# Half-swap of an 8192x8192 matrix: all row copies from GpSimd, each DMA over 8 rows a step

## The chip, the core and the metric

The kernel runs on one core of one Trainium2 chip. A core has five instruction engines (TensorE, VectorE, ScalarE, GpSimd and SyncE) and 16 DMA engines. This kernel computes nothing: its instruction engines only issue DMAs, and the DMA engines do the work.

The metric is device time in microseconds (us), from launch to end, as the median of several runs. Before the change it is 812.07 us, the median of 3 runs (811.68, 812.07, 814.06).

## What is computed

```python
x = np.random.randn(8192, 8192).astype(np.float32)
def reference(x):
    return np.fft.ifftshift(x)
```

With 8192 rows and columns, ifftshift moves every element by 4096 rows and 4096 columns, around the edges. So the four quadrants swap in pairs along the diagonals. Half a row (4096 float32 values, 16 KiB) stays together: the left half of output row r is the right half of input row (r + 4096) mod 8192, and the right half of output row r is the left half of that input row. A whole row is 32 KiB, each matrix 268.44 MB.

## The kernel before, in words

Nothing passes through on-chip memory: each DMA copies from the input in HBM to the output in HBM. `copy(queue, row, col, dims)` (L26) issues one DMA on the engine it is given as `queue`; the profile puts every DMA at L29, the line of that `dma_start`. Source and destination have the same three dimensions, `dims`, and differ only in their offset.

- The innermost dimension is the 4096 values of half a row: one packet of 16,384 bytes.
- The outermost dimension is 16 neighbouring rows (`ENGINES`), a row apart.
- Between them stands a dimension of `per` = 16 steps. Each step goes 16 rows back, so a DMA begins at the last 16 rows of its block and works towards its first ones.

So one DMA moves half a row of each of 16 x 16 = 256 rows (`rows`), which is 4 MiB in 256 packets. There are 64 DMAs: 32 blocks of 256 rows, each with a left and a right half.

The order of the work is written out by hand. The outer loop takes 4 blocks at a time and goes from the end of the matrix to its beginning. Within 4 blocks the left halves go in the order 3, 2, 1, 0, and the right halves in the order 1, 0, 3, 2: a left DMA and the right DMA issued beside it lie two blocks (512 rows) apart. Left halves are issued by SyncE (`nc.sync`, L38), right halves by ScalarE (`nc.scalar`, L39), 32 DMAs each. `ENGINES` is set ahead of the function, `per` in L23, and `dims` is `back` of L34.

No DMA depends on another. The framework gives each DMA one of eight completion semaphores in turn, four on each of the two engines. So from its fifth DMA on, each engine waits, before it issues, until the DMA four places earlier in its own order has landed. Eight DMAs are in flight, 4 left and 4 right. When a DMA is complete, each of its 16 parts has added one to the semaphore.

GpSimd does four small MEMSETs of constants at the start (L54, put there by the framework) and nothing else.

Of the kernel before, what the change touches and what calls it, by code (L numbers as in the profile page):

```python
# [1 line left out]

# [4 lines left out]


ENGINES = 16


@with_exitstack
def kernel(
    ctx: ExitStack,
    tc: tile.TileContext,
    x: bass.AP,
    out: bass.AP,
):
    nc = tc.nc
    R, C = x.shape  # L20
    hr = R // 2
    hc = C // 2
    per = 16  # L23
    rows = ENGINES * per

    def copy(queue, row, col, dims):  # L26

        src = (row + hr) % R * C + (col + hc) % C
        queue.dma_start(  # L29
            out=bass.AP(out.tensor, out.offset + row * C + col, dims),  # L30
            in_=bass.AP(x.tensor, x.offset + src, dims),
        )

    back = [[C, ENGINES], [-ENGINES * C, per], [1, hc]]  # L34

    for first in range(R - 4 * rows, -1, -4 * rows):
        for n in (3, 2, 1, 0):
            copy(nc.sync, first + n * rows + rows - ENGINES, 0, back)  # L38
            copy(nc.scalar, first + (n + 2) % 4 * rows + rows - ENGINES, hc, back)  # L39


# [1 line left out]
_INS = ['x']  # L43
_OUTS = [((8192, 8192), 'float32')]


def kernel(**inputs):
    import numpy as _np
    import concourse.bacc as _bacc
    import concourse.tile as _tile  # L50
    from concourse import mybir as _mybir
    from concourse.bass_utils import run_bass_kernel_spmd as _run

    nc = _bacc.Bacc("TRN2", target_bir_lowering=False, num_devices=1)  # L54
    arrays, args = {}, []
    for name in _INS:
        a = _np.ascontiguousarray(inputs[name])
        if a.dtype.kind in "iu":
            a = a.astype(_np.int64)
        arrays[f"in_{name}_dram"] = a  # L60
        args.append(nc.dram_tensor(f"in_{name}_dram", a.shape, _mybir.dt.from_np(a.dtype), kind="ExternalInput").ap())
    for i, (shape, dtype) in enumerate(_OUTS):
        dt = _mybir.dt.from_np(_np.dtype(dtype))
        args.append(nc.dram_tensor(f"out_{i}_dram", shape, dt, kind="ExternalOutput").ap())
    with _tile.TileContext(nc) as tc:
        kernel(tc, *args)
    r = _run(nc, [arrays], core_ids=[0])
    got = tuple(r.results[0][f"out_{i}_dram"] for i in range(len(_OUTS)))
    return got[0]
```

## Time and profile before

| | before |
|---|---|
| median of 3 runs | 812.07 us (811.68 to 814.06) |
| the profiled execution's own time | 813.9 us |
| span in that profile, first to last instruction | 812.1 us |
| bytes read from HBM, and written | 268.44 MB, 268.44 MB |
| packets | 17,408: 16,384 of 16 KiB, 1,024 of 4 bytes (semaphore updates) |
| first issue / first packet starts / last packet ends, in the span | 0.73 / 2.18 / 810.9 us |

The rows of the profile are read so. The "DMA" digits give, for each of 40 slices of the span, the mean busy share of the 16 DMA engines in tenths (9 is 90% or more). "GB/s" gives what was copied in that slice; each byte copied is read once and written once. A DMA queue's row ("q1", "q10") gives its packets, its bytes and the time of its packets as a share of 16 engines' span. An issue row gives how many DMAs an engine issued, their size, and the median time from the issue to the landing of the last byte. "SPq" and "ACTq" are the issuing sides of SyncE and ScalarE, and "POOL" is GpSimd. In the records of the trace, the 4-byte semaphore packets of q1 fall on the landings of SyncE's DMAs and those of q10 on ScalarE's, so q1 carries the left halves and q10 the right halves.

### The profile page before, as it was taken

To read this page: it belongs to the slowest core of one execution; us is meant where nothing else is said; L and a number is where in the kernel's file an instruction comes from. 1 tells how busy PE (TensorE), PEld (TensorE's weight loads), DVE (VectorE), ACT (ScalarE), POOL (GpSimd) and SP (SyncE) were. 2 spreads that over 40 slices of the span, in tenths; PEclk is the share of its full clock that TensorE was granted. 3 is DMA by queue.
4 is the path that set the end of the run, shared out by engine and by line. 5 is a ranking of instruction groups with operands and counts; after the bars stand their busy time and mean duration, and the time that the engine had idled before them with its cause. 6 is when DMAs were issued, how large, how long until landed. Compare 5 with 4: busy or idle time off the path is not lost. (4 is left out here: it accounts for less than half of the span.)

```text
span 812.1 us, 109 instructions
## 1 busy us (share of the span) xinstructions
POOL 0.2 (0%) x4
## 2 busy tenths in 40 slices
POOL 0000000000000000000000000000000000000000
DMA  9999999999999999999999999999999999999998
GB/s 306 332 329 337 333 332 335 328 324 337 329 336 337 332 334 334 334 336 331 332 329 330 337 328 334 339 331 333 332 320 333 330 331 330 336 332 337 334 333 286
DMA packets 17408, 268.44 MB, mean 331 GB/s; under 512 B 1024, under 2 KB 1024, under 8 KB 1024
## 3 DMA queue, kind: packets, MB, share of 16 engines
q1 hardware_dynamic: 8704, 134.22, 49.9%
q10 hardware_dynamic: 8704, 134.22, 49.1%
HBM read 268.44 MB, written 268.44 MB: 661 GB/s over the span
## 5 line engine op out<-in xcount | busy, mean ns | idle before, releaser
L54 POOL MEMSET const-bfloat16-1.0<- 128x1 bf16 x1 | 0.1, 102 | 0.0
L54 POOL MEMSET const-uint8-127<- 128x1 uint8 x1 | 0.1, 102 | 0.0
L54 POOL MEMSET const-float32-1.0<- 128x1 f32 x1 | 0.1, 99 | 0.0
L54 POOL MEMSET const-float32-0.0<- 128x1 f32 x1 | 0.1, 98 | 0.2 <-issue 0.2
## 6 DMA issues: line engine op xcount, KB each, us to landing
out_dram<-in_x_dram ACTq DMA_DIRECT2D x32, 4096.0 KB, 101.0
out_dram<-in_x_dram SPq DMA_DIRECT2D x32, 4096.0 KB, 101.0
```

The source lines that it names most:

```text
L54: nc = _bacc.Bacc("TRN2", target_bir_lowering=False, num_devices=1)
```

## The change

`ENGINES` goes from 16 to 8 and `per` from 16 to 32, so `rows` stays 256 and a DMA still moves 256 half rows, now as 32 steps of 8 neighbouring rows. All 64 DMAs are issued by GpSimd (`nc.gpsimd`), in one order: left half, right half, left half, and so on. Which blocks stand beside each other stays as it was. SyncE and ScalarE issue nothing.

```diff
-ENGINES = 16
+ENGINES = 8
...
-    per = 16
+    per = 32
     rows = ENGINES * per
...
     back = [[C, ENGINES], [-ENGINES * C, per], [1, hc]]
     for first in range(R - 4 * rows, -1, -4 * rows):
         for n in (3, 2, 1, 0):
-            copy(nc.sync, first + n * rows + rows - ENGINES, 0, back)
-            copy(nc.scalar, first + (n + 2) % 4 * rows + rows - ENGINES, hc, back)
+            copy(nc.gpsimd, first + n * rows + rows - ENGINES, 0, back)
+            copy(nc.gpsimd, first + (n + 2) % 4 * rows + rows - ENGINES, hc, back)
```

In the built kernel the DMAs of SyncE and ScalarE (16x16x4096, 32 on each) become 64 of 8x32x4096 on GpSimd. The first eight are issued without a wait; every later one waits for the DMA eight places before it, by eight semaphores in turn. So again eight are in flight, 4 left and 4 right, but the waits now stand in one order on one engine.

## The prediction

> **What bounds the kernel now.** I read the page from the top. Its first part has only four MEMSETs on GpSimd, 0.2 us; so the DMA rows carry everything.
>
> ```profile
> span 812.1 us, 109 instructions
> DMA  9999999999999999999999999999999999999998
> GB/s 306 332 329 337 333 332 335 328 324 337 329 336 337 332 334 334 334 336 331 332 329 330 337 328 334 339 331 333 332 320 333 330 331 330 336 332 337 334 333 286
> DMA packets 17408, 268.44 MB, mean 331 GB/s; under 512 B 1024, under 2 KB 1024, under 8 KB 1024
> q1 hardware_dynamic: 8704, 134.22, 49.9%
> q10 hardware_dynamic: 8704, 134.22, 49.1%
> HBM read 268.44 MB, written 268.44 MB: 661 GB/s over the span
> out_dram<-in_x_dram ACTq DMA_DIRECT2D x32, 4096.0 KB, 101.0
> out_dram<-in_x_dram SPq DMA_DIRECT2D x32, 4096.0 KB, 101.0
> ```
>
> The reader should see three things. The 16 DMA engines are busy in every slice (99.0% in sum, 49.9 + 49.1). The rate hardly moves: between the ramps of the first and last slice it lies between 320 and 339 GB/s. And no issue is late: 64 DMAs in 812.1 us are one per 12.7 us, and eight of them in flight make 101 us, which is the landing time in the last two rows; a DMA stands in a queue for nearly all of its life.
>
> Busy is not the same as at full speed. In the packet records a 16 KiB packet takes 0.608 us at the least, a third of the packets (33%) take under 0.616 us, the median is 0.726 and the mean 0.784 us. (These are read from the trace's record of each packet.) At 0.611 us throughout, 16 engines would need 16,384 x 0.611 / 16 = 626 us. So the engines are held up by something they share, by 28% on the mean. The bytes read and written together, 661 GB/s, pass through the HBM; I take that as the bound.
>
> The windows show that it is steady, and that the end is short:
>
> ```profile
> core 0: us, POOL busy (x), PEclk, DMA share, GB/s
> 0.00:20.00 20.00, 0.20 (x4) 1.00 0.91 307
> 100.00:200.00 100.00, 0.00 (x0) 1.00 0.99 331
> 400.00:500.00 100.00, 0.00 (x0) 1.00 1.00 332
> 700.00:800.00 100.00, 0.00 (x0) 1.00 0.99 333
> 807.00:812.10 5.10, 0.00 (x0) 1.00 0.43 138
> ```
>
> On the Trainium skill's page "HBM Reference", section "Specifications (TRN2)", one HBM domain gives about 716 GB/s. The 661 of the row are 92% of it; by that figure alone 536.9 MB would need an estimated 750 us, so it speaks against any large gain from a change of order, and no run here shows how near one can come.
>
> **The change, part by part.**
>
> *Which engines carry a DMA.* The whole change rests on it, and the trace of before does not show it: every DMA there has 16 rows a step and its 16 semaphore updates. The bounds are two. If left and right DMAs go to different eights of engines, all 16 stay in work, and nothing is lost. If both go to the same eight, each of these has 2 x 1024 packets at no less than 0.611 us, 1251 us. I take the first: in the trace the 16 rows of a step are dealt out so evenly that no engine falls behind (below), which is nearer to 64 DMAs shared by two eights than to one eight left idle.
>
> Here the skill speaks on both sides. "DMA: Bandwidth & Descriptors" says under "Rules for kernel authors" that an outermost dimension below 16 confines a DMA to at most that many engines, which speaks against the change; and under "Why a DMA increments its semaphore by 16 and not by 1" that SyncE's and ScalarE's DMAs take the lowest-numbered engines, but GpSimd's the next ones in turn from a moving cursor. By the first alone the sum would be 1251 us, by both together it is the one that follows. No row of this trace decides between them.
>
> *Removed: 32 issues on SyncE, 32 on ScalarE.* They were never late (each waited for a landing with three more of its DMAs queued), so taking them away gains nothing.
>
> *Added: 64 issues on GpSimd, and waits in one order.* GpSimd has nothing else to do after its MEMSETs. Behind a waiting issue stand all later DMAs of both halves. But DMA i+8 waits for DMA i, and when that one lands its engines still have three DMAs queued, 3 x 32 packets x 0.784 = 75 us. So a late half stops the other only when it is some 75 us behind. What GpSimd needs to prepare a DMA of 256 packets has no row. From below: no more than SyncE, whose first issue in the trace takes 0.67 us. From above: if each packet cost as much as a MEMSET (0.10 us), 25.6 us per DMA. Up to 12.7 us per DMA it is hidden, except before the first packets. Of the two I take the row of the same operation, 0.67 us, as the nearer; the other end is a rival.
>
> *Moved: left halves on eight engines, right halves on the other eight.* Today every engine carries both, so all 16 finish together: the 16 updates of a DMA lie 1.1 us apart at the first landing and 2 to 3 us at the last ones. That also says that no engine is slower than another by more than 3 us in 810. What differs is the kind of copy: a left packet takes 0.791 us, a right one 0.778. On halves of their own:
> - left: 49.9% x 2 x 812.1 = 810.5 us of packets on each of its eight engines
> - right: 49.1% x 2 x 812.1 = 797.5 us
> - gaps: packets fill 804.0 us of the 808.7 between the first packet's start (2.18) and the last one's end (810.9). The last updates lie 2 us apart, so up to 2 us of this are ragged ends; I keep 3 us of gaps per engine.
>
> The first left packet starts at 2.18 us, as now. In before the first right packet starts at 5.08 us, though both engines issued at 0.73: the second DMA comes 2.9 us behind the first. I keep that row for GpSimd's second DMA. Right ends at 5.08 + 800.5 = 805.6. By then left has done 803.4 of its 813.5 us, and 0.7 us more because for the first 2.9 us it was alone at 0.611 instead of 0.791. The last 9.4 us go at 0.611/0.791, that is in 7.3 us: 812.9. Then 1.2 us as now to the end of the span: 814.1, against 812.1.
>
> So the separation costs only 2 us, because the half that is left over speeds up. The cover here is the shared bound: what one half does not draw, the other gets.
>
> *The order of rows in flight.* Now 16 neighbouring half rows are in flight, from a mixture of a left and a right block; afterwards 8 and 8, for good. The records of before let the mixture be tested: with exactly 8 packets of q1 in flight the sum of the packets' rates is 335.5 GB/s, with 4 or 5 it is 331, with 11 or 12 it is 336. So a fixed mixture of 8 and 8 is worth under 1%. Whether 8 rows (256 KiB) apart or one queue instead of two per engine changes the rate has no row. The slices bound it: at the best slice's 339 GB/s the bytes take 791.9 us, at the mean's 331 811.0, at the worst's 320 838.9: from 19 us less to 28 us more. Nothing in the profile prefers an end; I take the middle rate, 329.5, which is 814.7 or 3.7 us more.
>
> **The sum.** 812.1 + 2.0 + 3.7 = 817.8 us of span. The profiled execution took 813.9 with a span of 812.1, but the median of the runs was 812.07, so I count the change on the median: 812.07 + 5.7 = 818 us, 0.7% more.
>
> **The rivals.**
> - *The rate falls* (8 rows apart, one queue per engine). For it: the mean packet is 0.784 and not 0.611, so order matters to what is shared. At the worst slice's rate: 814.1 + 27.9 = 842 us; if the halves also part a little more, 850. Chance 22%.
> - *The rate rises*, the case on the other side: each engine now makes one stream of rows in order instead of two interleaved ones, so packets get in each other's way less. Its place is the mean packet; 0.784 would have to fall to 0.765. At the best slice's rate: 814.1 - 19.1 = 795 us, at 1% over it 787. It decides from 333 GB/s on, where 268.44 MB take 5 us less than at 331, which makes good the 2 us of the halves and the 0.3% that can be told. Against it: in 800 us no slice stays above 339. Chance 33%.
> - *GpSimd becomes the bound.* It decides from 12.7 us per DMA; at 25.6 the time is 64 x 25.6 = 1638 us. Against it: 256 packets at under 50 ns each would do. Chance 5%.
> - *The change does not do what it says*: both halves on one eight of engines, 1251 us and 2.18 + 1.2 around it, 1255. Chance 5%.
>
> **How the numbers follow.** My forecast is that the rate stays within 2% and the halves cost 2 us: 810 to 826, at 818, chance 35%. A measurement of this kernel can tell about 0.3% from no change, that is 809.6 to 814.5: of the 35% some 12 lie within, 23 above. Faster 33% (the rate rises), same 12%, slower 23 + 22 + 5 + 5 = 55%. A range from 790 to 850 leaves out the two long cases (10%), some 7% of the gain and 3% of the loss.
>
> **What would show it.** Right: one queue for GpSimd with 268 MB, DMA digits still 9 in every slice, SPq and ACTq gone, and landings near 101 us for both kinds of DMA. The last slice should show the left half alone for under 10 us. GpSimd's issues should take about a microsecond or a few each, and the waits between them nearly all be for landings. The rate per slice settles the rest: 330 or so is my case, 320 or 339 the two rivals. Digits of 4 or 5 with half the rate would mean one eight of engines; digits that drop between DMAs, with no wait for landings, would mean GpSimd. If left and right drift apart by tens of us, the 75 us of cover are spent and my sum of the halves is wrong.

## The result and the profile after

The changed kernel takes 819.26 us (median of 4 runs, 817.76 to 820.89), the kernel before 812.82 us beside it (4 runs, 811.68 to 814.06). The ratio is 1.0078, 95% interval 1.0052 to 1.0105: slower by 0.8%, where 0.7% was forecast. The profiled execution took 819.35 us with a span of 817.6.

The page of the changed kernel, its first three parts and two rows of the last ones:

```profile
span 817.6 us, 109 instructions
...
DMA  8999999999999999999999999999999999999998
GB/s 276 316 331 323 320 327 328 325 331 331 327 339 335 328 330 334 328 335 333 337 334 334 333 333 331 338 327 336 329 335 334 334 334 327 338 333 335 330 334 275
DMA packets 33793, 268.51 MB, mean 328 GB/s; under 512 B 17408, under 2 KB 17408, under 8 KB 17408
...
q0 software_dynamic: 33792, 268.51, 99.3%
...
L29 POOL DMA_DIRECT2D out_dram<-in_x_dram x64 | 42.2, 661 | 674.6 <-DMA out_dram<-in_x_dram 673.7
...
out_dram<-in_x_dram POOLq DMA_DIRECT2D x64, 4096.0 KB, 100.6
```

The DMA digits are still 9 in nearly every slice, so all 16 engines are at work: left and right DMAs do use different eights (a packet's record does not name its engine, so this is read from the digits). One queue (q0) carries everything. An issue takes GpSimd 0.661 us (the mean in the L29 row), and 673.7 of the 674.6 us that GpSimd idles before issues are waits for landings: it is never the bound. Landings are at 100.6 us, as deep in the queue as before. What is new is the number of packets: 33,792, twice as many, for the same bytes. Of these, 17,408 are under 512 B, where there were 1,024.

The windows of the changed kernel (stretch, its length, GpSimd's busy time and instructions, clock, DMA share, GB/s) show where the time is lost:

```profile
0.00:4.00 4.00, 2.87 (x8) 1.00 0.21 45
4.00:8.00 4.00, 2.70 (x5) 1.00 0.84 283
...
20.00:100.00 80.00, 3.95 (x6) 1.00 1.00 323
100.00:200.00 100.00, 5.26 (x8) 1.00 1.00 328
...
400.00:500.00 100.00, 5.26 (x8) 1.00 1.00 333
...
700.00:800.00 100.00, 1.32 (x2) 1.00 1.00 334
```

Stretches of the kernel before:

```profile
0.00:4.00 4.00, 0.20 (x4) 1.00 0.53 188
4.00:8.00 4.00, 0.00 (x0) 1.00 0.99 356
...
20.00:100.00 80.00, 0.00 (x0) 1.00 0.99 333
```

From 400 us on, the changed kernel copies as fast as the one before (333 and 334 GB/s beside 332 and 333). It loses time in the first 8 us, where half of the engines start late, and in this execution also between 20 and 200 us. Counted in packets (how much later it has carried the same number of 16 KiB packets), it is 2.3 us behind after 8 us, 4.2 after 100, 5.8 after 300, and 4.6 after 800.

### The profile page after: what moved, and what is told of

It reads as the page before. It is cut to its first block, busy times and chain, and to the rows that moved or that the text cites. A ratio compares the mean times of both kernels' runs of the same rounds, so it can differ in the third digit from the quotient of the medians.

```text
span 817.6 us, 109 instructions
## 1 busy us (share of the span) xinstructions
POOL 42.4 (5%) x68
## 2 busy tenths in 40 slices
DMA packets 33793, 268.51 MB, mean 328 GB/s; under 512 B 17408, under 2 KB 17408, under 8 KB 17408
## 3 DMA queue, kind: packets, MB, share of 16 engines
q0 software_dynamic: 33792, 268.51, 99.3%
## 4 chain that ended last, share of the span: by engine, by line
another core or an unknown queue 77%; POOL 4%; DMA 4%; issue 2%; POOLq 0%; PEldq 0%
POOL out_dram L29 4%; DMA out_dram<-in_x_dram 4%; POOLq L66 0%; PEldq L66 0%
## 5 line engine op out<-in xcount | busy, mean ns | idle before, releaser
L29 POOL DMA_DIRECT2D out_dram<-in_x_dram x64 | 42.2, 661 | 674.6 <-DMA out_dram<-in_x_dram 673.7
## 6 DMA issues: line engine op xcount, KB each, us to landing
out_dram<-in_x_dram POOLq DMA_DIRECT2D x64, 4096.0 KB, 100.6
```

Source lines behind the costliest of these rows:

```text
L29: queue.dma_start(out=bass.AP(out.tensor, out.offset + row * C + col, dims), in_=bass.AP(x.tensor, x.offset + src, dims),)
```

## The experiments

All of these ran on chips on which the kernel before takes 822 us (821.9 to 822.4), 1.1% more than in the result above. So ratios are compared, each to the kernel before on the same chip in the same hours; 0.1% is 0.8 us. Where an expectation gives times, it means the times of the result above, and is put here as a ratio to 812.82 us. Single executions of the kernel before lay between 819.1 and 825.9 there, so a profile, which is one execution, can tell the place of a loss but not one of under 3 us in its total.

**Is the eight of engines decided by who issues?** Left halves on SyncE and right halves on ScalarE, with 8 rows a step:

```diff
-            copy(nc.gpsimd, first + n * rows + rows - ENGINES, 0, back)
-            copy(nc.gpsimd, first + (n + 2) % 4 * rows + rows - ENGINES, hc, back)
+            copy(nc.sync, first + n * rows + rows - ENGINES, 0, back)
+            copy(nc.scalar, first + (n + 2) % 4 * rows + rows - ENGINES, hc, back)
```

> 8 rows a step as in the changed kernel, but left halves issued by SyncE and right halves by ScalarE. If these two always take the same eight engines: half of the engines idle, 1245 to 1260 us, packets near 0.611 us. If they take halves in turn as GpSimd does: 810 to 822 us.

1249.85 us in its one run. Its page:

```profile
span 1248.1 us, 109 instructions
...
DMA  4555455554554555545555455455554554555544
...
q10 hardware_dynamic: 8448, 134.22, 25.1%
q1 hardware_dynamic: 8448, 134.22, 25.1%
```

Each queue is busy for a quarter of 16 engines, together a half. Each DMA has eight semaphore updates (512 small packets for 64 DMAs), so each is on eight engines, and with only eight busy in all both queues sit on the same eight. The time is 16,384 x 0.611 / 8 = 1251 us, to 0.1%. The mean packet now takes 0.611 us, as the shortest did before (0.608): with half of the engines no shared limit shows. So of the issuers tried, 8 rows a step only work on GpSimd, whose DMAs take the two eights in turn. This is the prediction's 1255 us rival, moved to the issuers where it holds.

**Is it the rows, or the queue?** All 64 DMAs on GpSimd with 16 rows a step (`ENGINES = 16`, `per = 16` in the changed kernel):

> All 64 DMAs on GpSimd as in the changed kernel, but with 16 rows a step as before, so each DMA is on all 16 engines. Theory A (the loss is the late and staggered start, 2.2 us, and a slow stretch up to 300 us, 3.5 us, that comes from left and right engines running in step): the slow stretch goes, 813 to 815.5 us. Theory B (the loss comes with GpSimd's queue, whatever the rows): 818 to 820 us, with the same slow stretch.

Ratio 1.0059, interval 1.0035 to 1.0084. As ratios theory A's times are 1.0002 to 1.0033 and theory B's 1.0064 to 1.0088: the interval leaves out A and reaches B. With 16 engines to each DMA, most of the loss is still there, and its profile is slow between 20 and 100 us too:

```profile
20.00:100.00 80.00, 3.34 (x6) 1.00 1.00 320
```

Left and right in step, theory A's reason, cannot be the cause here: every engine carries both. But this profile is the slowest of the kernel's twelve runs (832.35 us, median 826.63), and it stays slow later, at 325 and 326 GB/s up to 700 us.

**One queue without GpSimd.** The kernel before with `nc.scalar` replaced by `nc.sync`:

> The kernel before with all 64 DMAs on SyncE, one queue instead of two, nothing else changed. If one queue for each DMA engine costs rate, whoever issues: 817 us or more. Theories A and B both say no loss: 811 to 814 us.

Ratio 1.0043, interval 1.0023 to 1.0063. As ratios "no loss" was up to 1.0015 and a loss from 1.0051 on: the interval leaves out the first and reaches the second. So 3.5 us go with one queue on each engine instead of two, with the same 16-row DMAs and the same issuing engine for half of them. Neither theory A nor B had foreseen this.

One thing more changed than the call. The trace's rows for its issues (shortest, median and longest in ns, then the starts of the first and the last) and for their landings:

```profile
L29 SPq DMA_DIRECT2D out_dram<-in_x_dram x64: 592/11892/30113, 0.7 to 739.0; - x64
DMA to landing us min/median/max: 15.8/80.7/97.0
```

An issue of SyncE takes 11.9 us on the median, where it took 0.57 in the kernel before, as if its queue had room for only so many DMAs. Landings at 80.7 us with one DMA per 12.8 us mean that about six are in flight, not eight. The DMA engines do not run dry by it (on the mean they are without a 16 KiB packet for 1.2 us between 20 and 800 us, in the kernel before for 1.8), but the smaller number in flight is not excluded as a part of the 0.43%. In the run before this one, on GpSimd, eight are in flight (landings at 102.8 us), and the loss is there as well.

**Rows running in step.** The changed kernel with the right halves taken forwards:

```diff
+    forth = [[C, ENGINES], [ENGINES * C, per], [1, hc]]
...
-            copy(nc.gpsimd, first + (n + 2) % 4 * rows + rows - ENGINES, hc, back)
+            copy(nc.gpsimd, first + (n + 2) % 4 * rows, hc, forth)
```

> The changed kernel with the rows of the right halves taken forwards within each block, of the left ones backwards as before, so the two eights of engines meet the same distance of rows only for a moment. Theory A: the slow stretch between 40 and 300 us goes, 814 to 817 us. Theory B: no change, 818 to 821 us.

Ratio 1.0046, interval 1.0030 to 1.0062. As ratios theory A's times are 1.0015 to 1.0051 and theory B's 1.0064 to 1.0101, so the point lies with A and the interval leaves out B. But the interval overlaps the changed kernel's, and the slow stretch is weaker in its trace, not gone (325 GB/s from 20 to 100 us and 326 from 100 to 200, then 328 to 330), so the run by itself does not decide.

**The two kernels once more, with traces from one chip.**

> The kernel before once more, for a trace of it from the same chip as the others of this call. A ratio of 1.000 to the kernel before, within 0.2%.

Ratio 1.0002, interval 0.9983 to 1.0021.

> The changed kernel once more, beside the others on one chip. 0.5 to 1.05% slower than before. If the slow stretch up to 300 us belongs to it, its trace is 3 us or so further behind that of the kernel before at 200 us than at 40 us; if that was chance, the lag stays near 2 us until the end.

Ratio 1.0063, interval 1.0040 to 1.0085: the loss is there again. The windows of this second trace of the changed kernel:

```profile
0.00:4.00 4.00, 2.87 (x8) 1.00 0.23 49
4.00:8.00 4.00, 2.69 (x5) 1.00 0.83 291
...
20.00:100.00 80.00, 3.95 (x6) 1.00 1.00 329
100.00:300.00 200.00, 10.53 (x16) 1.00 1.00 329
300.00:500.00 200.00, 10.54 (x16) 1.00 1.00 329
```

And those of the kernel before on that chip:

```profile
20.00:100.00 80.00, 0.00 (x0) 1.00 1.00 327
100.00:300.00 200.00, 0.00 (x0) 1.00 1.00 328
300.00:500.00 200.00, 0.00 (x0) 1.00 1.00 329
```

The start is as it was in the first trace, to 0.1 us. The slow stretch from 20 to 200 us is gone (329 GB/s beside 327 and 328). Counted in packets the lag is 2.1 us at 40 us and 1.6 us at 200. By the expectation it was chance, then; but it comes back in other traces, and I return to it below. Theory A's reason, left and right engines in step, cannot be the whole of it: the 16-row kernels on SyncE and GpSimd show such a stretch too (321 and 320 GB/s from 20 to 100 us), and in them no engine carries one kind alone.

**One queue, or one kind of half in flight?** Two queues as before, each issuing left and right in turn:

```diff
-        for n in (3, 2, 1, 0):
-            copy(nc.sync, first + n * rows + rows - ENGINES, 0, back)
-            copy(nc.scalar, first + (n + 2) % 4 * rows + rows - ENGINES, hc, back)
+        for n in (3, 2):
+            copy(nc.sync, first + n * rows + rows - ENGINES, 0, back)
+            copy(nc.scalar, first + (n - 2) * rows + rows - ENGINES, 0, back)
+            copy(nc.sync, first + n * rows + rows - ENGINES, hc, back)
+            copy(nc.scalar, first + (n - 2) * rows + rows - ENGINES, hc, back)
```

> The kernel before with the order changed: SyncE and ScalarE each issue a left half, then each a right half, so two queues as before, but mostly one kind of half in flight, as with one queue. If one queue lost its 0.4% because the kinds are no longer mixed: 0.3 to 0.6% slower than before. If it lost it because there is one queue for an engine: within 0.2% of before.

Ratio 0.9992, interval 0.9974 to 1.0011: no loss that can be told, with two queues and eight DMAs in flight as before; so the mixture is not it.

**One queue, or one place of the matrix?** The kernel before with `first + n * rows` in both calls:

> The kernel before with left and right halves of the same block side by side (n in place of (n + 2) % 4): still two queues, but one block of 256 rows in flight instead of two. If one queue loses 0.4% because it works in one place of the matrix: 0.3 to 0.6% slower than before. If it loses it because it is one queue: within 0.2%.

Ratio 1.0011, interval 0.9993 to 1.0029: the point lies within 0.2%, though the upper end comes within 0.01% of the lowest that one place was to cost. The same edit in the changed kernel:

> The changed kernel with left and right halves of the same block side by side instead of 512 rows apart. If the place of the two halves decides the rate: more than 0.4% away from the changed kernel's 0.6 to 0.8% loss, to either side. If only the edges and the small packets count: 0.4 to 1.0% slower than before.

Ratio 1.0060, interval 1.0041 to 1.0080, beside 1.0063: the place of the halves does nothing that can be told.

**Two queues, one of them GpSimd's.** The kernel before with `nc.scalar` replaced by `nc.gpsimd`:

> The kernel before with the right halves issued by GpSimd instead of ScalarE, 16 rows a step: two queues, one of them GpSimd's. If all on GpSimd with 16 rows loses 0.6% because it is one queue: within 0.25% of before. If it loses it because GpSimd's queue is served worse: 0.25 to 0.6% slower.

Ratio 1.0016, interval 1.0001 to 1.0031. With a second queue most of the 0.59% is gone, although half of the bytes still come by GpSimd. The point lies inside the first expectation; the interval reaches a little into the second, so a small cost of GpSimd's queue is not excluded. After its last packet this profile takes 2.4 us to the end of the span, the kernel before 1.2; that difference is 0.15%, by this one trace nearly all of the 0.16%. But here, too, the number of DMAs in flight changed:

```profile
out_dram<-in_x_dram SPq DMA_DIRECT2D x32, 4096.0 KB, 157.0
out_dram<-in_x_dram POOLq DMA_DIRECT2D x32, 4096.0 KB, 204.0
```

With one DMA of each engine per 25.7 us, these landings mean about six in flight on SyncE's queue and eight on GpSimd's, 14 where the kernel before has eight. So a second queue and more DMAs in flight are not parted by this run.

**What the small packets cost.** The changed kernel with `ENGINES = 4` and `per = 64`:

> The changed kernel with 4 rows a step and 64 steps, so each DMA should be on four engines, with 256 rows to a DMA as before. If GpSimd's DMAs put one 4-byte packet on each engine that they do not use for each of its 16 KiB steps, there are 12 x 64 of them to a DMA, 49,152 instead of 16,384, 27 us of each engine's time instead of 9. If these packets cost what they take, 1.5 to 2.5% slower than before; if the others fill the time, only the later start of the third and fourth group adds (some 3 to 5 us): 1.0 to 1.4% slower.

Ratio 1.0163, interval 1.0135 to 1.0191. A line of its page and its first windows:

```profile
DMA packets 66561, 268.64 MB, mean 322 GB/s; under 512 B 50176, under 2 KB 50176, under 8 KB 50176
```

```profile
0.00:4.00 4.00, 2.83 (x8) 1.00 0.17 17
4.00:8.00 4.00, 4.00 (x6) 1.00 0.58 177
...
100.00:300.00 200.00, 13.44 (x16) 1.00 1.01 328
```

The small packets number 50,176: 1,024 semaphore updates and 64 x 12 x 64 = 49,152 others. By this count there is just one on each unused engine for each of the DMA's steps. The four groups of engines start one after another, and all 16 are at work only from 8.7 us on. From the packet records of the traces, all in us, the idle times being the mean time of the 16 engines without a 16 KiB packet:

| kernel | first packet starts | idle from there to 20 us | idle from 800 us to the last packet's end | from there to the end of the span | idle from 20 to 800 us | 16 KiB packets, sum / 16 | 4-byte packets, sum / 16 |
|---|---|---|---|---|---|---|---|
| before, first trace | 2.18 | 0.2 | 1.4 | 1.2 | 4.1 | 803.1 | 0.6 |
| after, first trace | 2.84 | 1.3 | 2.0 | 1.7 | 7.4 | 802.4 | 9.8 |
| before, second trace | 2.17 | 0.1 | 1.3 | 1.2 | 1.8 | 815.4 | 0.6 |
| after, second trace | 2.84 | 1.3 | 2.3 | 1.7 | 7.4 | 808.4 | 9.8 |
| 4 rows a step | 3.07 | 3.1 | 5.7 | 1.4 | 18.6 | 802.3 | 28.5 |

With 4 rows a step the first four columns are 8.5 us longer than before, 1.0%. The other 0.6% (0.3 to 0.9 by the interval) is left for the one queue and for small packets that take 28 us of each engine. So these do not cost what they take, which is 27.9 us more than before, 3.4%: the idle time of 20 to 800 us grows by 16.8 us, but the 16 KiB packets shrink by 13.1. What one engine does not draw, the others seem to get. The point, 1.63%, lies in the range that I gave for packets that cost what they take, yet not for that reason: the edges weigh more than I had expected, the small packets far less than their time.

**What the late start costs.** The first left and the first right DMA over 16 rows from SyncE and ScalarE, the other 62 as changed:

```diff
+    wide = [[C, 16], [-16 * C, 16], [1, hc]]
...
+            if first == R - 4 * rows and n == 3:
+                copy(nc.sync, first + n * rows + rows - 16, 0, wide)
+                copy(nc.scalar, first + (n + 2) % 4 * rows + rows - 16, hc, wide)
+                continue
```

> The changed kernel with its first left and its first right DMA issued by SyncE and ScalarE over 16 rows a step, the other 62 by GpSimd over 8 rows as in the changed kernel. The first packet should start at 2.2 us instead of 2.84, and the engines' idle time up to 20 us be near 0.2 us instead of 1.3: 1.8 us, so 0.3 to 0.6% slower than before where the changed kernel was 0.6 to 0.8%. If the start costs nothing in the end because the rate makes it good: 0.6 to 0.8% as the changed kernel.

Ratio 1.0064, interval 1.0041 to 1.0086. The start in its trace is mended:

```profile
0.00:4.00 4.00, 2.86 (x8) 1.00 0.55 172
4.00:8.00 4.00, 2.69 (x5) 1.00 0.97 348
```

The first packet starts at 2.19 us and the idle time up to 20 us is 0.2 us, yet the time is no better than the changed kernel's. Either the 1.8 us are made good later or they lie within the interval's 1.8 us to each side; this is not settled. No version tried is faster than the kernel before by more than the noise.

**The slow stretch, over all traces.** How much a kernel falls behind the kernel before between 20 and 200 us, counted in packets in one trace each (the changed kernel's first trace against the first one of before, all others against the second trace of before):

| one queue for an engine | us | two queues | us |
|---|---|---|---|
| after, first trace | 3.3 | left and right in turn on both | 0.4 |
| after, second trace | -0.2 | same block | 0.1 |
| 16 rows, SyncE | 1.3 | SyncE and GpSimd | -0.4 |
| 16 rows, GpSimd | 3.1 | | |
| right halves forwards | 1.3 | | |
| same block, 8 rows | 5.1 | | |
| 16-row start | 0.5 | | |
| 4 rows | 1.8 | | |

Six of eight traces with one queue lose 1 us or more there, on the mean of all eight 2.0 us; none of the three with two queues does. From 200 to 800 us the eight go from -3.1 to 3.6, on the mean 0.3, the three from -4.0 to -0.3. So a part of what one queue costs may have its place in the first 200 us. This is a lead and not shown: there is one trace of each kernel, two of the three largest figures come from unusually slow executions (832.35 us where the kernel's median was 826.63, and 832.3 where it was 827.58), and it was found by looking through the traces, not foreseen by an expectation.

## Why the prediction was right

The time, the sign and the size came out (818 forecast, 819.26 measured), but not every term is right. That it came so close is partly luck: 2.0 us stood for something that did not happen, about as much was missing for the edges, and the 3.7 us were the middle of bounds 47 us apart, with nothing to prefer it.

- **Two eights of engines, in turn.** Right, and the step on which all else stood: all digits stay 9. But the reason that I took from the trace, 16 rows dealt out evenly, did not bear on it: those were DMAs of SyncE and ScalarE, and just these two put 8 rows on one and the same eight (1249.85 us, the other bound).
- **GpSimd's issues at SyncE's 0.67 us.** Right: 0.661 us each, far below the 12.7 us where GpSimd would become the bound.
- **Waits in one order.** Right: landings at 100.6 us. Left and right land 1.8 us apart at the first pair and 2.4 at the last, so the 75 us of cover are hardly touched.
- **The second DMA 2.9 us behind the first.** Nearly: eight engines work alone from 2.84 us, the other eight join between 5.0 and 5.5. Not foreseen was that the first packet itself starts 0.66 us later. GpSimd issues at 1.33 us instead of 0.73, since it waits 0.9 us for a release first. From the waits of the changed kernel (what was waited for: us in total, times, the longest):

```profile
POOL out_dram L29 <- DMA out_dram<-in_x_dram: 673.7, 56, 23.6
POOL out_dram L29 <- PEq L66: 0.9, 1, 0.9
```

- **Left packets take longer, so the left half ends last and runs alone.** Wrong. In the changed kernel the last right DMA lands at 816.2 us, 2.4 after the last left one, and neither half runs alone for longer than that. The 0.791 and 0.778 us were no property of the halves. In the kernel with left on SyncE (q1) and right on GpSimd (q0) the order is the other way round, left shorter than right, in its queue rows:

```profile
q0 software_dynamic: 8704, 134.22, 50.2%
q1 hardware_dynamic: 8704, 134.22, 49.0%
```

  And with left and right halves in turn on both queues, SyncE's queue is still the longer (49.9% to 49.5%), so the difference went with the queue there.

  So the 2.0 us that I put there were for the wrong thing. (The sum has a slip of 0.1 us besides: 2.9 us alone at 0.611 instead of 0.791 are a lead of 0.85 us, not 0.7.) In their place stand the edges: 0.7 us to the first packet, 1.1 of idle engines at the start, 0.6 at the end and 0.5 after the last packet, 2.9 us in the first pair of traces. The experiment on the start says that not all of it need reach the end.
- **The order of rows and the number of queues, 3.7 us from the middle of two bounds.** The size is near, the reason only half known. Of the two things I put together there, the rows make no difference that can be told (16 rows 0.59%, 8 rows 0.63%; same block, opposite direction, same half), and the queue is what the ratios point to. One queue for each engine costs 0.43% on SyncE (3.5 us) and 0.59% on GpSimd; with a second queue it is 0.16%, 0.11% or nothing. By its trace, 1.3 us (0.15%) of GpSimd's 0.59% are edges (the first packet 0.5 us later, 0.8 us elsewhere), which leaves 0.44%, next to SyncE's 0.43%. Not parted from the queue are two things: how many DMAs are in flight, which changed in the run on SyncE and in the one on SyncE and GpSimd, and that with one queue of 16-row DMAs an engine has one DMA at a time to work on, where two queues give it two. How a second queue helps an engine that is busy anyway is not shown.
- **Small packets on the unused engines** were not in the sum at all. They take 9.2 us of each engine more than before. The whole loss is 5.2 us, so they cost less than they take; the likely reason is that the bound is shared. By the points of the ratios, one queue (3.5 us) leaves 1.7 of these 5.2 us (0.63% of 822) for them and the edges together; the intervals are too wide to part these.
- **Not the rival of a higher rate.** From 300 us on, eight ordered streams a half give 333 and 334 GB/s in the first trace and 329 in the second, 16 mixed ones 331 to 333 and 327 to 329.

## What to carry to other kernels

Here a copy held all DMA engines busy and was limited by something that they share, and rearranging the engines gained nothing in the middle; what the change moved most plainly was the edges, the first packets and the last ones. The edges of the old kernel can be read from its first and last few microseconds; those of another issuer are not in that profile, so give them a term of their own. A step of 8 rows worked only from the issuer whose DMAs took the engines in turn; from SyncE and ScalarE it left half of them idle. Two queues on each DMA engine were the better choice here: with one, some 0.4% was lost though the engines never ran dry. And when DMAs move from two queues to one, look at how many are then in flight: the code does not say it, the landing times do.

## What the runs showed of the hardware

- A DMA that GpSimd issues over 8 or 4 rows a step brings small packets of 4 bytes and 9 ns, one for each of its steps and each engine that it does not use, by their count: 16,384 and 49,152 of them here. SyncE's and ScalarE's DMAs over 8 rows do not: 16,384 packets of 16 KiB and 512 small ones in all.
- With all DMAs of 16 rows a step on SyncE, about six are in flight (landings at 80.7 us, one DMA per 12.8 us) and an issue takes 11.9 us on the median; with four at a time on it, in the kernel before, an issue takes 0.57 us. On GpSimd eight are in flight, and an issue takes 0.56 us.
- A 16 KiB copy within HBM takes an engine 0.611 us on the mean when only eight engines work (215 GB/s), and 0.78 to 0.80 us when all 16 do (323 to 334 GB/s in stretches of 80 us and more in the traces of the kernels before and after).
- The same kernel takes 812 us in the runs of the result and 822 on the three chips of the experiments, with packets 1.5% longer (815.4 to 803.1 us of packets for each engine). Why is not shown.
